# A two-layer hybrid backbone on one core: the order of its first loads, joined gate projections, and the list scheduler's price of a matmul

## The chip, the cores and the metric

One core of a Trainium2 chip runs the whole program in one launch. The metric is the device time of a run in microseconds; the median of several runs counts. Engines are named as in the profile: PE (TensorE, matmuls), PEld (its weight loads), DVE (VectorE), ACT (ScalarE), POOL (GpSimd) and SP (SyncE, which issues all DMAs here).

## What is computed

A stream of 256 latent tokens with a prefix of 256 context tokens passes two layers of width 1024. Cut to what matters here:

```
mod = silu(c) @ w_mod + b_mod                 # shift, scale, gate; context has its own
h   = rms(x) * (1 + scale) + shift            # 512 tokens
xa, ga, q, k, v, gb, qd, kvd, kr, gc, gm = split(h @ w_in)
ya = gated linear recurrence of xa            # both directions
yb = chunked retention of q, k, v             # both directions, 4 heads
yc = latent attention from qd, kvd, kr        # 8 heads
z  = sum over branches of sigmoid(gm_i) * ((y_i * silu(g_i)) @ w_down_i)
x  = x + gate * (z @ w_out)                   # the last layer: latent tokens only
```

## The kernel before

**Arithmetic.** Each operand of a large matmul is split into two fp32r parts, a rounded one and a remainder: `split` (lines 506 to 508) writes the rounded part on ACT and the remainder on DVE. `mm3` (520) then issues three matmuls for each product: high by high, high by low, low by high. Weights come as tiles of 128 x 1024 through `load_raw` and `load` (527 to 537): a DMA into a `raw` tile (5 slots), then the split into `whi` and `wlo` (5 slots each). The normalized activations live in `hh` and `hl`, each 128 x 8 x 512 (channel block, token).

**The order of the work.** The program is not emitted as it is written. `Recorder` (151) records every operation of all five engines with its dependencies and the price that `_cost` (412) gives it; `schedule` (224) then plays a list scheduler over these prices: on each engine the first ready operation in program order whose tiles have slots starts, and the order so found is emitted by line 368, which is why every row of the profile has that line. Tiles of a pool (`t2`, 21 slots of 128 x 1024; `sm`, 6 of 128 x 512; `mm`, the 8 PSUM banks) may be taken out of turn only if `RESERVE` slots stay free and the tile is at most `WINDOW` ahead (lines 39 and 40, test at 282 to 284). SP is one queue in the order of the list.

**The start** (lines 1167 to 1194). `mod_pe` (586) computes one of four blocks of the modulation: four DMAs of 512 KB into `raw` tiles, eight matmuls with a stationary operand of 32 columns, a copy out of the bank on ACT, four small matmuls with `sel`, and the DVE steps of `put_columns`. `load_x` brings 128 tokens, and `norm_begin` (652) squares, sums and scales them. `norm_channels` (678) transposes one block of channels of all tokens, applies scale and shift and splits the result into `hh` and `hl`. `kv_project` (753) multiplies two channel blocks by their latent weights of 320 columns into four banks. The program order is: block 0 of the modulation, four token loads, block 1, then for each of four pairs of channel blocks the normalization, the projection, and the modulation two blocks ahead.

**Projections for latent tokens only.** `proj` (689) computes 128 channels for all 512 tokens, or, with `lat`, for the 256 latent tokens: 24 matmuls of 256 columns. In layer 1 `silu_gate` (697; kinds gc, ga, gb, 8 each) and `ret_head` (1080; q, 2 for each of 4 heads) call it so. The readers take the result out of the bank: tanh on ACT and a product on DVE in `silu_gate`, the rope products on DVE in `ret_head`. `merge_rows` (996) keeps two `sm` tiles of gates while it runs 48 matmuls.

Of the kernel before, what the change touches and what calls it, by code (L numbers as in the profile page):

```python
# [36 lines left out]
LATENCY = (650.0, 300.0, 200.0)  # L37
SWITCH = 600
WINDOW = {"t2": 12, "sm": 24, "st": 24, "mm": 32}
RESERVE = {"t2": 3, "sm": 1, "st": 4, "mm": 1}  # L40
NRAW = 5
NHI = 5
# [108 lines left out]
class Recorder:  # L151
# [72 lines left out]
    def schedule(self):  # L224
# [34 lines left out]
        while left:  # L259
            progressed = True  # L260
            while progressed:
                progressed = False
                for e in engines:
                    if busy[e] > t:
                        continue
                    w = wait[e]
                    while w and w[0][0] <= t:
                        _, pr, k, op = heapq.heappop(w)
                        heapq.heappush(avail[e], (pr, k, op))
                    a = avail[e]  # L270
                    hold = []
                    pick = None
                    while a:
                        item = heapq.heappop(a)
                        op = item[2]
                        ok = True
                        need = {}
                        for b in op.allocs:
                            if b.live:
                                continue  # L280
                            need[b.tag] = need.get(b.tag, 0) + 1
                            spare = RESERVE.get(b.tag, 0) if b.seq > nxt[b.tag] + need[b.tag] - 1 else 0
                            if free[b.tag] < need[b.tag] + spare or b.seq > nxt[b.tag] + WINDOW.get(b.tag, 0):
                                ok = False
                        if ok and pick is not None:
                            if not switch(op):
                                hold.append((pick.prio, id(pick), pick))
                                pick = op
                                break
                            ok = False  # L290
                        elif ok:
                            pick = op
                            if not switch(op):
                                break
                            limit = op.prio + SWITCH
                            continue
                        hold.append(item)
                        if pick is not None and item[0] > limit:
                            break
                    for item in hold:  # L300
                        heapq.heappush(a, item)
                    if pick is None:
                        continue
                    op = pick
                    for b in op.allocs:
                        if not b.live:
                            b.live = True
                            free[b.tag] -= 1
                            q = self.tags[b.tag]["queue"]
                            while nxt[b.tag] < len(q) and q[nxt[b.tag]].live:  # L310
                                nxt[b.tag] += 1
                    cost = op.cost
                    if switch(op):
                        cost += 1283.0
                        table[0] = op.table
                    op.start = t
                    busy[e] = t + cost
                    op.end = t + cost + op.lag
                    order.append(op)
                    left -= 1  # L320
                    evn += 1
                    heapq.heappush(events, (busy[e], evn, None))
                    evn += 1
                    heapq.heappush(events, (op.end, evn, op))
                    for s in op.succs:
                        if s.engine == e and e != "SP":
                            s.ready = max(s.ready, busy[e] + SELF[e])
                        else:
                            s.ready = max(s.ready, op.end + _latency(e, s.engine))
                        s.npred -= 1  # L330
                        if s.npred == 0:
                            heapq.heappush(wait[s.engine], (s.ready, s.prio, id(s), s))
                            evn += 1
                            heapq.heappush(events, (s.ready, evn, None))
                    progressed = True
            if not left:
                break
            if not events:
                self.stuck(nxt, free, wait, avail)
            t2, _, op = heapq.heappop(events)  # L340
            t = max(t, t2)
            batch = [op]
            while events and events[0][0] <= t:
                batch.append(heapq.heappop(events)[2])
            for op in batch:
                if op is not None:
                    for b in op.bufs:
                        b.users -= 1
                        if b.users == 0:
                            free[b.tag] += 1  # L350
# [61 lines left out]
def _cost(engine, method, args, kwargs):  # L412
    out = args[0]
    n = _size(out) if isinstance(out, View) else 0
    if engine == "PE":
        if method == "transpose":
            return 107.0, 0.0
        passes = 1 if args[1].buf.dtype == F32R else 4
        return max(passes * n / 2.4, 27.0 if passes == 1 else 211.0) + 2.7, 0.0
    if engine == "SP":  # L420
        size = 4 * int(np.prod(args[1].shape))
        return size / 370.0 + 30.0, 2000.0
    psum = any(isinstance(x, View) and x.buf.psum for x in args[1:])
    if engine == "ACT":
        ptr = sum(isinstance(kwargs.get(k), View) for k in ("scale", "bias"))
# [22 lines left out]
def tile_hybrid(ctx, tc, ins, out):  # L448
# [8 lines left out]
        return p  # L457

    const = pool("const", 1)
    pool("hp", 1, ["hh", "hl"])  # L460
    pool("raw", NRAW)
    pool("whi", NHI)
    pool("wlo", NLO)
# [12 lines left out]
    def big(dt=F32R):  # L476
        return rec.tile("t2", [128, 1024], dt)
# [52 lines left out]
        return raw[:, 0:n]  # L530

    def load(src, n=1024):
        raw = load_raw(src, n)
        hi = rec.tile("whi", [128, 1024], F32R)[:, 0:n]
        lo = rec.tile("wlo", [128, 1024], F32R)[:, 0:n]
        split(hi, lo, raw)
        return hi, lo
# [45 lines left out]
        ng = col(l, "ng", s.start, 2).unsqueeze(2).to_broadcast([128, 2, 2])  # L583
        V.scalar_tensor_tensor(gt[:, s, :], src[:, 2:4, :], 1.0, ng, op0=ALU.add, op1=ALU.mult)

    def mod_pe(l, c, gt, sh):
        ps = bank()
        for kp in range(4):
            raw = load_raw(ins["wmod"][l, 4 * c + kp])
            for kk in range(2):  # L590
                k = 2 * kp + kk
                q = 32 * (k % 4)
                T.matmul(ps[q:q + 32, :], cz[:, k, :], raw[:, kk * 512:(kk + 1) * 512], start=k < 4, stop=k >= 4)
# [90 lines left out]
        V.tensor_scalar(hf[:, 256:512], pt[:, 256:512], gt[:, kt, 0:1], sh[:, kt, 0:1], op0=ALU.mult, op1=ALU.add)  # L684
        split(hh[:, kt, :], hl[:, kt, :], hf)

    hcur = [None, None]

    def proj(ps, l, kind, j, lat):
        hh, hl = hcur  # L690
        hi, lo = unit(l, kind, j)
        c = slice(256, 512) if lat else slice(0, 512)
        ps = ps[:, 0:256] if lat else ps
        mm3(ps, [(hi[:, k * 128:(k + 1) * 128], lo[:, k * 128:(k + 1) * 128], hh[:, k, c], hl[:, k, c]) for k in range(8)])
        return ps

    def silu_gate(l, kind, j):
        ps = proj(bank(), l, kind, j, l == 1)
# [34 lines left out]
    class Latents:  # L733
# [3 lines left out]
            self.q0 = 0 if l == 0 else 256  # L737
            self.kv_banks, self.q_banks = {}, {}

        def project(self, src, n, banks, tts, kps):  # L740
            hh, hl = hcur
            for kp in kps:
                hi, lo = load(ins[src][self.l, kp], 2 * n)
                for tt in tts:
                    if tt not in banks:
                        banks[tt] = bank()
# [3 lines left out]
                        w = slice(kk * n, (kk + 1) * n)  # L750
                        mm3(banks[tt][:, 0:n], [(hh[:, k, s], hl[:, k, s], hi[:, w], lo[:, w])], start=k == 0, stop=k == 7)

        def kv_project(self, kps):
            self.project("wkv", 320, self.kv_banks, range(NTT), kps)

        def q_project(self, kps):
            self.project("wqd", 384, self.q_banks, self.qtt, kps)
# [237 lines left out]

    def merge_rows(l, br, zr, first, last):
        names = {0: ("gmc", "dc"), 1: ("gma", "da"), 2: ("gmb", "db")}[br]
        hh, hl = hcur
        ys = ys_out[br]
        for c in range(2):  # L1000
            cs_ = slice(c * 512, (c + 1) * 512)
# [57 lines left out]
        return dt  # L1059

    def ret_pair(l, p):
        hh, hl = hcur
        banks = [bank() for _ in range(NTT)]
        for kp in range(4):
            hi, lo = unit(l, "v", 4 * p + kp)
# [100 lines left out]

    xt = []
    mods = {}
    hh = rec.tile("hh", [128, 8, 512], F32R)
    hl = rec.tile("hl", [128, 8, 512], F32R)  # L1170
    hcur[0], hcur[1] = hh, hl

    def new_mod():
        return rec.tile("gt", [128, 8, 2], F32), rec.tile("sh", [128, 8, 2], F32)
# [1 line left out]
    gt, sh = new_mod()  # L1176
    xn = {}

    def load_x(tt):
        x = big(F32)  # L1180
        S.dma_start(x, ins["xin"][tt])
        xn[tt] = norm_begin(x)

    lat = Latents(0, None)
    mod_pe(0, 0, gt, sh)
    for tt in range(NTT):
        load_x(tt)
    mod_pe(0, 1, gt, sh)
    for c in range(4):
        for kt in (2 * c, 2 * c + 1):  # L1190
            norm_channels(xn, kt, gt, sh, hh, hl)
        lat.kv_project((c,))
        if c < 2:
            mod_pe(0, c + 2, gt, sh)
    lat.tabs = rope_tables(0)
    sp = cload("sp", [128, DEPTH, 24])
    rrope = cload("rrope", [128, 2, 256])
# [41 lines left out]
    for l in range(DEPTH):  # L1239
# [43 lines left out]
        if l == 0:  # L1283
            for tt in tts:
                x = big(F32)
                S.dma_start(x, ins["xin"][tt])
                xt.append(x)
            hh = rec.tile("hh", [128, 8, 512], F32R)
            hl = rec.tile("hl", [128, 8, 512], F32R)

        def residual(half, tt, ps):
            hs = slice(half * 512, (half + 1) * 512)
# [25 lines left out]
                for half in range(2):  # L1318
                    norm_half(xn, tt, half, gt, sh, hh, hl)
        if l == 0:  # L1320
            hcur[0], hcur[1] = hh, hl
            lat = Latents(1, rope_tables(1))
            lat.kv_project(range(4))

# [113 lines left out]
```

## Time and profile before

| | |
|---|---|
| runs | 1401.82, 1403.86, 1404.72 us; median 1403.86 |
| profiled execution | 1403.3 us; its span 1401.4 us |
| PE busy | 1381.6 us (99%) |
| DVE busy | 1018.2 us (73%) |
| ACT busy | 792.1 us (57%) |
| mean DMA rate over the span | 121 GB/s |

The span runs from the first to the last instruction. Matmuls are pipelined: the duration of one contains the wait for the one ahead, so the distance between starts, not the duration, is what one costs in a row.

### The profile page before, as it was taken

The numbers are of one execution on the slowest core, as the hardware profiler recorded it, in microseconds if no ns is written. First come the engines' busy times: TensorE is split into PE (matmuls) and PEld (weight loads), VectorE is DVE, ScalarE is ACT, GpSimd is POOL, SyncE is SP. The second block draws the span as 40 slices with busy tenths as digits, with TensorE's granted clock in tenths as the row PEclk, the third lists the DMA queues.
The fourth block names the chain that finished last, engine by engine and source line by source line (L and its number), as shares of the span: only waits on it lengthen the run. The fifth ranks groups of instructions, "written<-read, shape, count | busy, mean of one in ns | idle before, by whom it ended". The sixth has DMA issues, their size and how long they took to land.

```text
span 1401.4 us, 19672 instructions
## 1 busy us (share of the span) xinstructions
PE 1381.6 (99%) x7182; PEld 1178.8 (84%) x7182; DVE 1018.2 (73%) x2035; ACT 792.1 (57%) x1565; POOL 83.6 (6%) x109
## 2 busy tenths in 40 slices
PE   6999999999999999999999999999999999999998
PEld 4888888888888888888888888999888888889887
DVE  3589887667668655574785765899777888878654
ACT  3585664676668323153433225877586877954442
POOL 0131110000000000010000001322000000000000
PEclk9999999999999999999999999999999999999999
DMA  8512212333333433413344452332343444556562
GB/s 313 189 48 78 68 46 68 98 89 99 91 114 120 150 87 104 134 60 105 108 140 151 124 185 72 116 99 91 99 123 118 154 130 139 162 176 203 145 185 76
DMA packets 51071, 170.17 MB, mean 121 GB/s; under 512 B 6048, under 2 KB 7840, under 8 KB 50976
## 3 DMA queue, kind: packets, MB, share of 16 engines
q1 hardware_dynamic: 50976, 168.93, 38.9%
q8 instruction: 56, 0.92, 0.3%
q14 instruction: 39, 0.32, 0.1%
HBM read 167.86 MB, written 1.05 MB: 121 GB/s over the span
## 4 chain that ended last, share of the span: by engine, by line
PE 93%; DVE 3%; DMA 2%; ACT 1%; issue 0%; SPq 0%; POOL 0%; ACTq 0%; POOLq 0%
PE mm L368 93%; DVE sm L368 1%; DVE t L368 1%; DVE wlo L368 1%; DMA raw<-in_wkv_dram 1%; ACT t L368 1%; DMA t<-in_xin_dram 1%; DMA raw<-in_wmod_dram 0%; DVE st L368 0%; DMA raw<-in_wqd_dram 0%; ACT whi L368 0%; SPq L368 0%; ACT sm L368 0%; POOL st L368 0%; ACT hh L368 0%
## 5 line engine op out<-in xcount | busy, mean ns | idle before, releaser
L368 ACT CAST whi<-raw 128x1024 fp32r<-128x1024 f32 (+4 forms) x280 | 275.6, 995 | 347.0 <-PE mm L368 294.8
L368 DVE TENSOR_TENSOR wlo<-raw,whi 128x1024 fp32r<-128x1024 f32 (+4 forms) x280 | 318.6, 1143 | 148.7 <-ACT whi L368 146.6
L368 PE MATMUL mm<-hh,whi 128*128 128x512 f32 (+1 forms) x960 | 349.7, 364 | 0.0
L368 PE MATMUL mm<-hh,wlo 128*128 128x512 f32 (+1 forms) x960 | 348.5, 363 | 0.0
L368 PE MATMUL mm<-hl,whi 128*128 128x512 f32 (+1 forms) x960 | 348.1, 363 | 0.0
L368 PE MATMUL mm<-whi,t 128*128 128x512 f32 (+1 forms) x656 | 208.3, 383 | 0.4 <-DVE t L368 0.4
L368 PEld LDWEIGHTS mm<-hl,whi 128*128 128x128 f32 x960 | 181.2, 189 | 26.7
L368 PEld LDWEIGHTS mm<-hh,wlo 128*128 128x128 f32 x960 | 181.2, 189 | 26.6
L368 PEld LDWEIGHTS mm<-hh,whi 128*128 128x128 f32 x960 | 181.2, 189 | 26.4
L368 PE MATMUL mm<-t,whi 128*128 128x512 f32 x512 | 160.1, 390 | 0.1
L368 POOL TENSOR_TENSOR st<-st,nhalf 128x2 f32<-128x2 f32 (+2 forms) x102 | 82.7, 817 | 1230.0 <-DVE st L368 1211.6
L368 PE MATMUL mm<-t,t 128*128 128x256 f32 (+1 forms) x912 | 153.8, 310 | 0.5 <-ACT t L368 0.5
L368 PEld LDWEIGHTS mm<-t,t 128*128 128x128 f32 x912 | 129.4, 190 | 11.7 <-DVE t L368 1.2
L368 PEld LDWEIGHTS mm<-whi,t 128*128 128x128 f32 x656 | 121.8, 188 | 18.8 <-DVE t L368 0.6
L368 PE MATMUL mm<-wlo,t 128*128 128x512 f32 (+1 forms) x328 | 125.6, 383 | 0.0
L368 PE MATMUL mm<-whi,hh 128*128 128x512 f32 (+2 forms) x336 | 123.8, 369 | 0.1
L368 PE MATMUL mm<-wlo,hh 128*128 128x512 f32 (+2 forms) x336 | 123.4, 368 | 0.0
L368 PE MATMUL mm<-whi,hl 128*128 128x512 f32 (+2 forms) x336 | 123.1, 369 | 0.2 <-DVE hl L368 0.2
L368 PEld LDWEIGHTS mm<-t,whi 128*128 128x128 f32 x512 | 95.8, 188 | 20.9 <-ACT t L368 0.8
L368 ACT ACTIVATE sm<-mm 128x128 f32<-128x128 f32 (+4 forms) x266 | 93.1, 366 | 21.3 <-PE mm L368 18.2
L368 ACT CAST t<-sm 128x256 fp32r<-128x256 f32 (+1 forms) x128 | 60.3, 487 | 71.2 <-DVE sm L368 67.7
L368 PE MATMUL mm<-t,wlo 128*128 128x512 f32 x256 | 99.6, 389 | 0.0
(108 smaller groups left out, 1738.4 us busy)
## 6 DMA issues: line engine op xcount, KB each, us to landing
raw<-in_wu_dram SPq DMA_DIRECT2D x224, 512.0 KB, 3.6
raw<-in_wmod_dram SPq DMA_DIRECT2D x48, 512.0 KB, 4.2
t<-in_xin_dram SPq DMA_DIRECT2D x8, 512.0 KB, 7.4
raw<-in_wup_dram SPq DMA_DIRECT2D x8, 512.0 KB, 4.0
raw<-in_wlru_dram SPq DMA_DIRECT2D x16, 256.0 KB, 3.2
raw<-in_wqd_dram SPq DMA_DIRECT2D x8, 384.0 KB, 3.3
raw<-in_wup_dram SPq DMA_DIRECT2D x8, 384.0 KB, 3.4
raw<-in_wkv_dram SPq DMA_DIRECT2D x8, 320.0 KB, 5.4
```

Of the source, the lines that this page charges most:

```text
L368: getattr(eng[op.engine], op.method)(*[r(x) for x in op.args], **{k: r(v) for k, v in op.kwargs.items()})
```

## The change

Four parts. (1) At the start the four token loads come first; then for each block its four modulation loads, now into slots of `t2`, and its latent weights, and then the block's work: modulation, two channel blocks, projection. (2) A projection with `lat` uses one tile `hx` that holds `hh` and `hl` side by side: the high weights meet both halves in one matmul of 2 x 256 columns, the low weights meet `hh` in one of 256, and the two halves of the bank are added by a copy on ACT and an addition on DVE into an `sm` tile. (3) `_cost` prices a one-pass matmul at columns / 2.4 + 13.3 ns with a floor of 108, counts a stationary operand of up to 32 columns as one pass, and a DMA byte at 1/400 ns. (4) Banks before number 24 are taken out of turn only if four stay free.

```diff
+FIRST = {"mm": 4}
-spare = RESERVE.get(b.tag, 0) if b.seq > nxt[b.tag] + need[b.tag] - 1 else 0
+spare = (FIRST if b.tag == "mm" and b.seq < 24 else RESERVE).get(b.tag, 0) if b.seq > nxt[b.tag] + need[b.tag] - 1 else 0
...
-        passes = 1 if args[1].buf.dtype == F32R else 4
-        return max(passes * n / 2.4, 27.0 if passes == 1 else 211.0) + 2.7, 0.0
+        passes = 1 if args[1].buf.dtype == F32R or _size(args[1]) <= 32 else 4
+        return max(passes * (n / 2.4 + 13.3), 108.0 if passes == 1 else 211.0), 0.0
     if engine == "SP":
         size = 4 * int(np.prod(args[1].shape))
-        return size / 370.0 + 30.0, 2000.0
+        return size / 400.0 + 30.0, 2000.0
...
-    pool("hp", 1, ["hh", "hl"])
+    pool("hp", 1, ["hx"])
...
-        c = slice(256, 512) if lat else slice(0, 512)
-        ps = ps[:, 0:256] if lat else ps
-        mm3(ps, [(hi[:, k * 128:(k + 1) * 128], lo[:, k * 128:(k + 1) * 128], hh[:, k, c], hl[:, k, c]) for k in range(8)])
-        return ps
+        if not lat:
+            mm3(ps, [(hi[:, k * 128:(k + 1) * 128], lo[:, k * 128:(k + 1) * 128], hh[:, k, :], hl[:, k, :]) for k in range(8)])
+            return ps
+        both = ps.rearrange("p (s t) -> p s t", s=2)
+        for k in range(8):
+            w = slice(k * 128, (k + 1) * 128)
+            if k > 0:
+                T.matmul(ps[:, 0:256], lo[:, w], hh[:, k, 256:512], start=False, stop=False)
+            T.matmul(both, hi[:, w], hx[:, :, k, 256:512], start=k == 0, stop=k == 7)
+            if k == 0:
+                T.matmul(ps[:, 0:256], lo[:, w], hh[:, k, 256:512], start=False, stop=False)
+        s = small()[:, 0:256]
+        A.copy(s, ps[:, 256:512])
+        V.tensor_tensor(s, ps[:, 0:256], s, op=ALU.add)
+        return s
...
-            raw = load_raw(ins["wmod"][l, 4 * c + kp])
+            raw = wm[c][kp]
...
-    mod_pe(0, 0, gt, sh)
     for tt in range(NTT):
-        load_x(tt)
-    mod_pe(0, 1, gt, sh)
+        xs.append(big(F32))
+        S.dma_start(xs[tt], ins["xin"][tt])
+    wm = {}
     for c in range(4):
+        wm[c] = [big(F32) for _ in range(4)]
+        for kp in range(4):
+            S.dma_start(wm[c][kp], ins["wmod"][0, 4 * c + kp])
+        wkv = load_raw(ins["wkv"][0, c], 640)
+        if c == 0:
+            for tt in range(NTT):
+                xn[tt] = norm_begin(xs[tt])
+        mod_pe(0, c, wm, gt, sh)
         for kt in (2 * c, 2 * c + 1):
             norm_channels(xn, kt, gt, sh, hh, hl)
-        lat.kv_project((c,))
-        if c < 2:
-            mod_pe(0, c + 2, gt, sh)
+        lat.kv_project((c,), {c: wkv})
```

`project` takes the weights loaded ahead through `split_raw`, the second half of `load`.

## Rows read from the trace of the kernel before

**Rows 1.** The page, part 4: the chain that ended last, by engine.

```profile
PE 93%; DVE 3%; DMA 2%; ACT 1%; issue 0%; SPq 0%; POOL 0%; ACTq 0%; POOLq 0%
```

**Rows 2.** Busy time by stretch: stretch, length, engines (instructions), PE clock, DMA share, GB/s.

```profile
0.00:48.30 48.30, 34.26 (x194) 21.59 (x194) 19.67 (x55) 20.03 (x35) 3.16 (x11) 0.93 0.87 316
...
90.00:131.00 41.00, 40.12 (x227) 33.49 (x225) 39.69 (x128) 25.91 (x94) 8.87 (x9) 1.00 0.28 79
131.00:1396.00 1265.00, 1264.73 (x6509) 1083.98 (x6510) 929.10 (x1760) 714.45 (x1321) 59.87 (x74) 1.00 0.38 117
```

**Rows 3.** Groups of PE by form, 0 to 48.3 us: count, busy us, mean ns.

```profile
L368 PE MATMUL mm<-raw,cz 128*32 128x512 f32 x64 | 13.3, 729 | 7.8 <-DMA raw<-in_wmod_dram 6.2 <-ACT hh L368 1.6
L368 PE MATMUL mm<-whi,hh 128*128 128x320 f32 x24 | 7.8, 325 | 0.1
...
L368 PE MATMUL mm<-ident,t 128*128 128x128 f32 x26 | 5.2, 360 | 4.3 <-DVE st L368 3.0 <-ACT sm L368 1.3
L368 PE MATMUL mm<-sel,sm 128*128 128x2 f32 x32 | 4.8, 270 | 1.2 <-ACT sm L368 1.2
```

**Rows 4.** Timeline of the opening: start us, duration us, instruction, count, idle before.

```profile
23.02 1.14 ACT L368 CAST hh<-sm 128x512 fp32r<-128x512 f32 x2 [0.91 <-DVE sm L368]
...
32.96 0.58 ACT L368 COPY sm<-mm 128x512 f32<-128x512 f32 x1 [2.86 <-PE mm L368]
...
34.57 0.95 PE L368 MATMUL mm<-sel,sm 128*128 128x2 f32 x8
...
36.02 0.54 DVE L368 TENSOR_SCALAR sm<-mm,gt,sh 128x256 f32<-128x256 f32 x1
36.04 0.31 PE L368 MATMUL mm<-whi,hh 128*128 128x320 f32 x1
...
37.07 0.31 PE L368 MATMUL mm<-wlo,hh 128*128 128x320 f32 x1
...
37.45 1.92 PE L368 MATMUL mm<-raw,cz 128*32 128x512 f32 x16
```

**Rows 5.** Timeline, weight loads that waited for the first modulation tiles.

```profile
7.34 0.19 PEld L368 LDWEIGHTS mm<-raw,cz 128*32 128x32 f32 x4 [0.97 <-DMA raw<-in_wmod_dram]
...
9.89 0.18 PEld L368 LDWEIGHTS mm<-raw,cz 128*32 128x32 f32 x4 [1.08 <-DMA raw<-in_wmod_dram]
```

**Rows 6.** Busy time by stretch of 5 us; the last two numbers are DMA share and GB/s.

```profile
10.00:15.00 5.00, 2.02 (x12) 1.11 (x10) 1.33 (x4) 3.72 (x7) 1.11 (x2) 0.84 1.03 417
15.00:20.00 5.00, 5.00 (x26) 3.80 (x27) 2.34 (x8) 2.16 (x6) 1.10 (x2) 0.50 1.02 403
20.00:25.00 5.00, 3.37 (x24) 1.47 (x18) 3.03 (x5) 2.35 (x4) 0.00 (x0) 0.97 0.69 240
...
40.00:45.00 5.00, 2.85 (x15) 2.09 (x16) 3.64 (x6) 4.07 (x8) 0.00 (x0) 1.00 1.00 349
```

**Rows 7.** Timeline of the SP queue: start us, us, DMA issues and their count.

```profile
20.57 1.75 SPq L368 DMA_DIRECT2D raw<-in_wmod_dram  x4
...
33.47 5.41 SPq L368 DMA_DIRECT2D raw<-in_wkv_dram  x2
```

**Rows 8.** Timeline of PE: matmuls of 512 columns (310 us), of 256 (1044 us).

```profile
309.71 0.39 PE L368 MATMUL mm<-hh,whi 128*128 128x512 f32 x1
...
311.52 0.39 PE L368 MATMUL mm<-hh,wlo 128*128 128x512 f32 x1
...
1044.01 0.28 PE L368 MATMUL mm<-hl,whi 128*128 128x256 f32 x1
...
1050.97 0.28 PE L368 MATMUL mm<-hh,wlo 128*128 128x256 f32 x1
```

**Rows 9.** Groups by form, whole span: 256-column reads of a bank, ACT and DVE.

```profile
L368 ACT ACTIVATE sm<-mm 128x256 f32<-128x256 f32 x32 | 12.4, 388 | 3.2 <-PE mm L368 3.1
...
L368 DVE TENSOR_TENSOR t<-mm,t 128x256 fp32r<-128x256 f32 x56 | 23.2, 417 | 1.8 <-ACT t L368 1.5
```

**Rows 10.** Busy time by stretch, in the attention of layer 1.

```profile
940.00:960.00 20.00, 20.00 (x129) 18.23 (x128) 19.39 (x54) 14.96 (x55) 3.54 (x4) 1.00 0.43 133
```

More of the change, by code (lines that the diff above doesn't have):

```diff
@@ L532, in load, with split_raw @@
     def load(src, n=1024):
-        raw = load_raw(src, n)
+        return split_raw(load_raw(src, n), n)
+    def split_raw(raw, n):
         hi = rec.tile("whi", [128, 1024], F32R)[:, 0:n]
@@ L584, in put_columns, with mod_pe @@
         V.scalar_tensor_tensor(gt[:, s, :], src[:, 2:4, :], 1.0, ng, op0=ALU.add, op1=ALU.mult)
-    def mod_pe(l, c, gt, sh):
+    def mod_pe(l, c, wm, gt, sh):
         ps = bank()
         for kp in range(4):
-            raw = load_raw(ins["wmod"][l, 4 * c + kp])
+            raw = wm[c][kp]
             for kk in range(2):
@@ L685, in norm_channels @@
         split(hh[:, kt, :], hl[:, kt, :], hf)
-    hcur = [None, None]
+    hcur = [None, None, None]
     def proj(ps, l, kind, j, lat):
-        hh, hl = hcur
+        hh, hl, hx = hcur
         hi, lo = unit(l, kind, j)
-        c = slice(256, 512) if lat else slice(0, 512)
-        ps = ps[:, 0:256] if lat else ps
-        mm3(ps, [(hi[:, k * 128:(k + 1) * 128], lo[:, k * 128:(k + 1) * 128], hh[:, k, c], hl[:, k, c]) for k in range(8)])
-        return ps
+        if not lat:
[13 more added lines that the diff above has]
+        return s
     def silu_gate(l, kind, j):
@@ L738, in __init__, with project @@
             self.kv_banks, self.q_banks = {}, {}
-        def project(self, src, n, banks, tts, kps):
-            hh, hl = hcur
+        def project(self, src, n, banks, tts, kps, raws=None):
+            hh, hl, hx = hcur
             for kp in kps:
-                hi, lo = load(ins[src][self.l, kp], 2 * n)
+                hi, lo = split_raw(raws[kp], 2 * n) if raws else load(ins[src][self.l, kp], 2 * n)
                 for tt in tts:
@@ L751, in project, with kv_project @@
                         mm3(banks[tt][:, 0:n], [(hh[:, k, s], hl[:, k, s], hi[:, w], lo[:, w])], start=k == 0, stop=k == 7)
-        def kv_project(self, kps):
-            self.project("wkv", 320, self.kv_banks, range(NTT), kps)
+        def kv_project(self, kps, raws=None):
+            self.project("wkv", 320, self.kv_banks, range(NTT), kps, raws)
         def q_project(self, kps):
@@ L997, in merge_rows @@
         names = {0: ("gmc", "dc"), 1: ("gma", "da"), 2: ("gmb", "db")}[br]
-        hh, hl = hcur
+        hh, hl, hx = hcur
         ys = ys_out[br]
@@ L1061, in ret_pair @@
     def ret_pair(l, p):
-        hh, hl = hcur
+        hh, hl, hx = hcur
         banks = [bank() for _ in range(NTT)]
@@ L1168, in tile_hybrid @@
     mods = {}
-    hh = rec.tile("hh", [128, 8, 512], F32R)
-    hl = rec.tile("hl", [128, 8, 512], F32R)
-    hcur[0], hcur[1] = hh, hl
+    hx = rec.tile("hx", [128, 2, 8, 512], F32R)
+    hh, hl = hx[:, 0], hx[:, 1]
+    hcur[0], hcur[1], hcur[2] = hh, hl, hx
     def new_mod():
@@ L1177, in tile_hybrid @@
     xn = {}
[L1179 to L1182, printed above, removed]
     lat = Latents(0, None)
-    mod_pe(0, 0, gt, sh)
+    xs = []
     for tt in range(NTT):
-        load_x(tt)
-    mod_pe(0, 1, gt, sh)
+        xs.append(big(F32))
+        S.dma_start(xs[tt], ins["xin"][tt])
+    wm = {}
     for c in range(4):
+        wm[c] = [big(F32) for _ in range(4)]
[6 more added lines that the diff above has]
+        mod_pe(0, c, wm, gt, sh)
         for kt in (2 * c, 2 * c + 1):
             norm_channels(xn, kt, gt, sh, hh, hl)
-        lat.kv_project((c,))
-        if c < 2:
-            mod_pe(0, c + 2, gt, sh)
+        lat.kv_project((c,), {c: wkv})
     lat.tabs = rope_tables(0)
@@ L1287, in tile_hybrid @@
                 xt.append(x)
-            hh = rec.tile("hh", [128, 8, 512], F32R)
-            hl = rec.tile("hl", [128, 8, 512], F32R)
+            hx = rec.tile("hx", [128, 2, 8, 512], F32R)
+            hh, hl = hx[:, 0], hx[:, 1]
         def residual(half, tt, ps):
@@ L1320, in tile_hybrid @@
         if l == 0:
-            hcur[0], hcur[1] = hh, hl
+            hcur[0], hcur[1], hcur[2] = hh, hl, hx
             lat = Latents(1, rope_tables(1))
```

## The prediction

> **What bounds the kernel now.** I read the chain of waits first, by engine [rows 1]: matmuls are 93% of it, so only what shortens TensorE's work or its gaps counts. Then a table of stretches [rows 2]. From 131 to 1396 us TensorE is busy 1264.73 of 1265 us: no order of the list can win anything there, only lose. The first 48.3 us are different: 34.26 us busy, at a granted clock of 0.93, which is 2.4 GHz but for some 6.8 us at 1.2 GHz. From 90 to 131 us VectorE is busy 39.69 of 41 us, and the chain runs over it.
>
> "Busy" overstates TensorE in the opening, as matmuls overlap, so I count work instead. By 48.33 us it has done 64 records of the modulation matmuls, 24 x 3 = 72 of the latent projection (the row shown is one of three alike), 32 of the selector and 26 of the 32 transposes [rows 3]. Undisturbed steps, from starts in rows 4: 16 modulation records take 1.92 us, 0.12 each; seven steps of 320 columns take 37.07 - 36.04 = 1.03, 0.147 each; 8 selector records take 0.95, 0.12 each; a transpose stands at 0.107 in the price function, and I take that. Sum: 64 x 0.12 + 72 x 0.147 + 32 x 0.12 + 26 x 0.107 = 7.7 + 10.6 + 3.8 + 2.8 = 24.9 us. TensorE is 48.3 - 24.9 = **23.4 us behind** what it could have done, and from there on it hardly stops.
>
> Why: modulation tiles come at 1.25 to 1.3 us (the weight loads at 7.34 and 9.89 us that waited for them are two tiles apart [rows 5]). The DMA engines are full until 20 us at 403 to 417 GB/s, then fall to 240 [rows 6]. The SP queue shows it: the third four modulation loads start only at 20.57 us, the last latent weights between 33.47 and 38.9 [rows 7]. All go through the five raw slots.
>
> **The opening, changed.** No load is added. The four token loads go ahead of the first modulation loads, each block's four modulation loads and its latent weights follow, and the modulation tiles take slots of the 21-slot pool instead of the raw ones. The table loads (rope, decay) fall behind all blocks; their readers come after the blocks too. On SP nothing in the row needs a slot that is late: 4 token tiles, 4 normalized ones and 16 modulation tiles are 24 for 21 slots, so the last three loads wait for token tiles, which are free some 3 us after they land at about 10 (square, power, scaling; an estimate), when more than 13 us of transfers are still queued. Token loads 5 us earlier bring the squares (ACT), powers (POOL) and scalings (DVE) forward into idle time.
>
> Bytes: 20 x 0.524 + 4 x 0.328 = 11.8 MB. The fourth 0.524 MB load landed at 9.89 us; the other 9.7 MB at 0.524/1.275 = 0.411 MB per us take 23.6 us. Last modulation tile at 32.7, last latent weights at 33.5 us. Behind that tile come four records (0.5), the copy (0.58), the selectors (0.95), 0.50 until the affine step starts, the affine step (0.54), and one rounding (1.14/2 = 0.57) [rows 4]: 3.6 us, with handoffs and other work on these engines 4.8. So the last block's projection starts at 37.5 us, and the query weights, next in the queue, keep TensorE fed from there. Its work by then: 24.9 plus six transposes (0.6) = 25.5. It is 12.0 us behind instead of 23.4: **11.4 us less**. Bounds: with 18 of the first query matmuls of 384 columns, at the planner's own 173 ns, filling the wait, 14.5 less; with transfers at 349 GB/s, the rate at 40 to 45 us [rows 6], 27.8 instead of 23.6 us, 4.2 less gain; and if the lower clock level falls on two blocks' projections (48 x 0.147 = 7 us) with nothing to hide it, 7 us less. So 0 to 14.5.
>
> I keep 10 of the 11.4: the stretch of 90 to 131 us, where VectorE is full, should move forward as a whole, as VectorE has over half of the first 48.3 us free [rows 2], but the late blocks now press more work of ACT and VectorE into fewer microseconds.
>
> **Joined gates.** `proj` with lat serves 32 projections in layer 1 (gc, ga, gb, 8 each, and 8 for q). Each has 24 matmuls of 256 columns; 58 steps from 1044.01 to 1050.97 us are 0.120 us each. The joined form has 8 of 256 and 8 of 512 columns; eight steps from 309.71 to 311.52 are 0.226 each [rows 8]. Per pair of joined matmuls 2 x 0.120 - 0.226 = 0.014 us, x 256 = **3.5 us less** on the bounding engine. The moving operand now reads two runs, one in each half of `hx`, which no row shows: if that costs what separate matmuls cost, 0 is gained; nothing suggests more. I take 2.8, near the row's end.
>
> The Trainium skill (TensorE: Matmul & The Clock Gate, Back-to-back issue gap) puts the gap of isolated matmuls at columns / 2.4 plus about 2.5 ns: by that, joining saves only 2.5 ns each, an estimated 0.6 us in all. The trace differs: 0.120 and 0.226 us leave 13 ns fixed, and the measurement decides.
>
> Added: 32 copies out of a bank (0.388 us by the 32 reads alike) and 32 additions (0.417) [rows 9]: 12.4 us on ACT and 13.3 on VectorE. TensorE doesn't wait for these while banks are free; the bank is free after the addition, about as early as before, when tanh and the product read it. Cover: in 940 to 960 us VectorE is 19.39 of 20 us busy [rows 10]. Eight of the projections lie in that region, 8 x 0.42 = 3.3 us; without cover all of it would count. I take 0.5, since TensorE has other projections to run. Net of gates: 2.3 less.
>
> **Prices.** The planner took a 512-column matmul for 216 ns and now takes 226.6, a 256-column one for 109 and now 120: the rows' values. A modulation matmul falls from 856 to 227 (two records, 0.24). The floor of 108 touches no matmul here (the one-pass ones have 256 columns or more) and a transpose stays at 107. So the opening is no longer planned with 32 x 0.63 = 20 us of matmul time that isn't there, which lets the better loads take effect. Between 131 and 1396 us it can't gain; a worse order can lose. I take 0 and leave the loss to the range and the last rival. The bank reserve of 4 before number 24 keeps four banks for the latent sums: no instruction. `hx` for `hh` and `hl`: the same bytes, the same last readers: 0.
>
> **Sum.** The profiled execution took 1403.3 us (1401.4 of span, 1.9 around it). 1403.3 - 10 - 2.3 = 1391.0; the runs' median is 0.56 above the profiled time: **1391.5 us**. Its own range is 1386 to 1396.
>
> **Rivals.**
> *Slow stream or cold engine.* The opening's loads run at 349 GB/s, or half clock stretches the blocks: 4 to 6 us of the 10 are lost, 1396.5. For it: the later full stretch of the queue is at that rate; against: 10 us at 403 to 417. Chance 0.12. The Trainium skill (DMA: Bandwidth & Descriptors, Specifications) gives about 358 GB/s as HBM's share per core, an estimated 3.5 us more for the 9.7 MB; the trace, one core alone at 417, disagrees so far.
>
> *VectorE takes it back.* The opening ends 10 us earlier, but the stretch to 131 us is held by VectorE's 39.69 of 41 us and ends where it did, or two or three earlier. Then 1403.9 - 2.3 - 1.5 = 1400. Against: its work there depends on what TensorE delivers earlier. Chance 0.12.
>
> *Small tiles run out (slower).* The joined projection holds a small tile, the query pair of a retention head two, beside three of its rope step: five of six. In layer 1 the merge holds two through 48 matmuls, 48 x 0.226 = 10.8 us. If TensorE's projections then stand with no free bank at each of the four heads, up to 4 x 10.8 = 43 us are lost; it decides from 12.3/4 = 3.1 us per head. At 4 us per head: 1391.5 + 16 = 1407.5. Against: the list knows the tiles and can put other projections there. Chance 0.08.
>
> *The change misses its aim.* The list puts the new loads in a row, but order elsewhere gives up what the opening gains: 1401 to 1404. Chance 0.08.
>
> **Numbers.** The forecast has 0.6. The range 1384 to 1401 takes in the first two rivals and the bounds (14.5 + 3.5 less on one side). A measurement of this kernel can tell about 0.2%, 2.8 us, from no change: faster is below 1401.05, slower above 1406.7. Faster: 0.6 + 0.12 + two thirds of 0.12 = 0.80; slower 0.08; the rest, 0.12, within.
>
> **What would show it.** Right: tokens land by 10 us, the DMA stays near 410 GB/s to 32 us, the last modulation tile lands near 33 us and the last block's projection starts near 37; joined pairs step 0.226 + 0.120; stretches after 131 us keep TensorE at 100%; the layer-1 stretch is 2 to 3 us shorter. Wrong: SP standing on the 21-slot pool before 25 us; steps of 0.24 or more at joined matmuls; TensorE idle behind VectorE in 80 to 130 us; idle TensorE at the four retention heads of layer 1.

## The result: slower, and the profile after

The changed kernel takes 1413.13 us (median of 4 runs, 1412.91 to 1415.39), the kernel before 1403.54 beside it: a ratio of 1.0073, with a 95% interval of 1.0055 to 1.0090. The forecast was 1391.5, with a range of 1384 to 1401: wrong in sign. The profiled execution spans 1410.5 us, 9.1 more than before.

The page of the changed kernel, busy time by engine and, from its part 4, the chain by engine:

```profile
PE 1382.9 (98%) x6926; PEld 1161.2 (82%) x6926; DVE 1027.7 (73%) x2067; ACT 800.3 (57%) x1597; POOL 83.9 (6%) x109
...
PE 78%; DVE 9%; ACT 7%; DMA 3%; issue 1%; POOL 1%; SPq 0%; ACTq 0%; DVEq 0%; POOLq 0%
```

TensorE has 256 matmuls fewer (6926 for 7182), as the joined gates make it. But the chain, 93% matmuls before [rows 1], is 78% now: ACT and VectorE hold 16% of it. The stretches of the changed kernel show where:

```profile
0.00:48.30 48.30, 36.04 (x222) 24.05 (x223) 22.46 (x60) 22.38 (x38) 3.61 (x11) 1.00 0.90 338
...
90.00:131.00 41.00, 38.26 (x223) 32.44 (x222) 39.62 (x141) 24.69 (x89) 7.89 (x8) 1.00 0.22 66
...
200.00:600.00 400.00, 398.86 (x1832) 330.44 (x1831) 264.30 (x407) 213.41 (x297) 2.78 (x5) 1.00 0.34 104
...
850.00:1250.00 400.00, 396.96 (x2076) 338.67 (x2075) 331.42 (x680) 306.54 (x643) 32.77 (x38) 1.00 0.39 120
```

From 90 to 131 us TensorE has lost 1.9 us of busy time against [rows 2], and in the body, where nothing was idle before, it now is: 1.1 us of 400 and 3.0 of 400. It waits in many short gaps. What it waited for between 200 and 1390 us, first in the kernel before, then in the changed one (total us, times, longest):

```profile
PEld mm L368 <- ACT t L368: 0.8, 2, 0.4
PEld mm L368 <- DVE t L368: 0.5, 1, 0.5
PEld mm L368 <- DVE sm L368: 0.4, 2, 0.2
```

```profile
PEld mm L369 <- ACT t L369: 6.5, 12, 1.1
PEld mm L369 <- DVE t L369: 4.8, 12, 0.9
PEld mm L369 <- ACT sm L369: 3.3, 5, 1.8
```

One of these gaps in the changed kernel's timeline:

```profile
454.64 0.68 DVE L369 TENSOR_TENSOR sm<-sm,t 128x512 f32<-128x512 f32 x1
454.77 0.19 PEld L369 LDWEIGHTS mm<-hx,wlo 128*128 128x128 f32 x1
454.99 0.39 PE L369 MATMUL mm<-hx,wlo 128*128 128x512 f32 x1
...
455.36 0.62 ACT L369 CAST t<-sm 128x512 fp32r<-128x512 f32 x1 [2.29 <-DVE sm L369]
456.03 0.19 PEld L369 LDWEIGHTS mm<-t,whi 128*128 128x128 f32 x1 [1.07 <-ACT t L369]
456.03 0.50 PE L369 MATMUL mm<-t,whi 128*128 128x512 f32 x1 [0.65 <-ACT t L369]
```

A product leaves VectorE at 455.32, ACT rounds it until 455.98, and the matmul that the list has put next on TensorE starts at 456.03, 0.8 us late.

Busy time hides most of this, so the working below uses **lag**, the measure of the prediction's opening: the time t less the undisturbed steps of all matmuls begun before t. The steps are the medians between starts in a row in the traces: 0.227 us for 512 columns, 0.174 for 384, 0.147 for 320, 0.120 for 256, 0.109 for a transpose and 0.112 for a selector; for a modulation record it is a mean, 16 of them in 1.92 us, 0.120. They add up to 1366.2 us before and 1362.9 with joined gates. Each column is one profiled execution. Lag in us, for the main kernels of the next section ("changed, old matmul price" is f1_oldmm there, "fastest" h1_ahead):

| at us | before | changed | opening alone | joined alone | prices alone | changed, old matmul price | fastest |
|---|---|---|---|---|---|---|---|
| 50 | 23.6 | 19.4 | 24.6 | 24.5 | 22.6 | 19.4 | 15.8 |
| 80 | 23.9 | 19.5 | 25.8 | 25.3 | 24.8 | 19.6 | 15.9 |
| 200 | 27.8 | 28.0 | 30.9 | 29.3 | 33.0 | 23.7 | 20.0 |
| 600 | 28.5 | 31.0 | 30.8 | 29.9 | 36.5 | 23.8 | 20.0 |
| 850 | 28.8 | 31.1 | 31.1 | 30.2 | 36.8 | 23.9 | 20.2 |
| 1350 | 30.2 | 42.6 | 32.5 | 32.6 | 45.7 | 26.5 | 22.9 |

The changed kernel is 4.4 us ahead at 80 us, has given that back by 200, and loses 14.6 us from 200 to 1350 where the kernel before loses 2.4. With 3.3 us less work, 12.4 - 3.3 = 9.1 us: the difference of the spans. The joined gates alone stand 1.4 us worse than the kernel before at 80 us already, though they lie in layer 1: in that execution the granted clock was 0.91 over the first 60 us, in the kernel before 0.94.

### The profile page after: what moved, and what is told of

Its sections match the earlier page's. It is cut to its first block, busy times and chain, and to the rows that moved or that the text cites. A ratio compares the mean times of both kernels' runs of the same rounds, so it can differ in the third digit from the quotient of the medians.

```text
span 1410.5 us, 19235 instructions
## 1 busy us (share of the span) xinstructions
PE 1382.9 (98%) x6926; PEld 1161.2 (82%) x6926; DVE 1027.7 (73%) x2067; ACT 800.3 (57%) x1597; POOL 83.9 (6%) x109
## 3 DMA queue, kind: packets, MB, share of 16 engines
HBM read 167.86 MB, written 1.05 MB: 120 GB/s over the span
## 4 chain that ended last, share of the span: by engine, by line
PE 78%; DVE 9%; ACT 7%; DMA 3%; issue 1%; POOL 1%; SPq 0%; ACTq 0%; DVEq 0%; POOLq 0%
PE mm L369 78%; DVE t L369 4%; ACT t L369 3%; DVE sm L369 3%; DVE wlo L369 2%; ACT whi L369 2%; DMA t<-in_wmod_dram 1%; ACT sm L369 1%; DVE st L369 1%; POOL st L369 1%; DMA sm<-in_grope_dram 1%; DMA raw<-in_wu_dram 0%; ACT L369 0%; DMA t<-in_xin_dram 0%; DMA raw<-in_wmod_dram 0%
## 5 line engine op out<-in xcount | busy, mean ns | idle before, releaser
L369 PE MATMUL mm<-hx,whi 128*128 128x512 f32 x1664 | 534.3, 393 | 1.7 <-ACT sm L369 0.9
L369 PEld LDWEIGHTS mm<-hx,whi 128*128 128x128 f32 x1664 | 309.8, 188 | 62.8 <-DVE t L369 1.4
L369 PE MATMUL mm<-hx,wlo 128*128 128x512 f32 (+1 forms) x960 | 343.1, 363 | 0.0
L369 PEld LDWEIGHTS mm<-hx,wlo 128*128 128x128 f32 x960 | 180.4, 188 | 28.5
L369 PE MATMUL mm<-whi,hx 128*128 128x512 f32 (+2 forms) x672 | 197.0, 369 | 1.5 <-ACT hx L369 1.4
L369 PEld LDWEIGHTS mm<-whi,hx 128*128 128x128 f32 x672 | 122.8, 188 | 21.5 <-ACT hx L369 3.9
L369 PE MATMUL mm<-wlo,hx 128*128 128x512 f32 (+2 forms) x336 | 122.9, 368 | 0.1
L369 PEld LDWEIGHTS mm<-t,whi 128*128 128x128 f32 x512 | 95.2, 188 | 25.8 <-ACT t L369 5.2
L369 ACT ACTIVATE sm<-mm 128x128 f32<-128x128 f32 (+4 forms) x242 | 85.7, 375 | 16.7 <-PE mm L369 16.3
L369 ACT ACTIVATE sm<-mm,st 128x256 f32<-128x256 f32 (+2 forms) x86 | 49.8, 592 | 47.2 <-DVE st L369 38.7
L369 DVE SCALAR_TENSOR_TENSOR t<-raw,cf,t 128x512 f32<-128x512 f32 x98 | 69.6, 743 | 9.6 <-DMA raw<-in_wmod_dram 9.5
```

Source lines behind the costliest of these rows:

```text
L369: getattr(eng[op.engine], op.method)(*[r(x) for x in op.args], **{k: r(v) for k, v in op.kwargs.items()})
```

## The experiments

All times are medians in us; the ratio is to the kernel before in the same set of runs, with its 95% interval.

| run | time | ratio |
|---|---|---|
| opening alone (e1_open) | 1406.32 | 1.0019 (1.0009 to 1.0028) |
| joined gates alone (e2_join) | 1400.40 | 0.9980 (0.9970 to 0.9989) |
| prices and bank reserve alone (e3_price) | 1418.05 | 1.0098 (1.0083 to 1.0113) |
| all but the prices (e4_noprice) | 1404.18 | 1.0000 (0.9991 to 1.0010) |
| all, old matmul price (f1_oldmm) | 1396.77 | 0.9942 (0.9927 to 0.9957) |
| matmul and DMA price alone (f2_pm) | 1426.80 | 1.0154 (1.0138 to 1.0169) |
| all, handoff to TensorE doubled (f3_lat) | 1405.72 | 1.0016 (1.0006 to 1.0026) |
| all, half the fixed part (f4_half) | 1401.24 | 0.9981 (0.9971 to 0.9991) |
| all, matmul prices x 0.953 (g1_uniform) | 1399.69 | 0.9969 (0.9958 to 0.9980) |
| all, ACT and VectorE prices x 1.05 (g2_others) | 1399.33 | 0.9966 (0.9955 to 0.9978) |
| all, fixed part 13.0 (g4_jit) | 1413.21 | 1.0068 (1.0053 to 1.0083) |
| f1_oldmm, projection a block later (h1_ahead) | 1392.56 | 0.9922 (0.9907 to 0.9937) |
| all, only the modulation's price new (k1_pz) | 1396.18 | 0.9935 (0.9918 to 0.9951) |
| h1_ahead, matmul price 5% lower still (k2_low) | 1397.95 | 0.9952 (0.9937 to 0.9966) |

**Which part.** Each of the three parts alone on the kernel before, and the change without its prices.

Opening alone: the hunks of the start, `split_raw` and `FIRST`.

> The kernel before with the new opening (loads in a row, work by block, the bank reserve) alone; old prices, separate gate matmuls. Theory P (the new prices' order loses what the rest gains): the opening alone keeps its gain, about 4 us, so near 1399. Theory J (the joined gates lose it in layer 1): the same, 1399, as neither is in this kernel. Theory O (the opening's gain is taken back by VectorE before 200 us, as in the changed kernel): 1403, no change.

Joined gates alone: the hunk of `proj`, with `hx`.

> The kernel before with the joined gate projections alone. Theory J: slower by 5 to 8 us, 1409 to 1412, all of it behind 850 us. Theory P: faster by 1 to 3 us, 1401 to 1402, since TensorE's work is 3 us less. Theory O: the same as P.

Prices alone:

```diff
+FIRST = {"mm": 4}
...
-        passes = 1 if args[1].buf.dtype == F32R else 4
-        return max(passes * n / 2.4, 27.0 if passes == 1 else 211.0) + 2.7, 0.0
+        passes = 1 if args[1].buf.dtype == F32R or _size(args[1]) <= 32 else 4
+        return max(passes * (n / 2.4 + 13.3), 108.0 if passes == 1 else 211.0), 0.0
...
-        return size / 370.0 + 30.0, 2000.0
+        return size / 400.0 + 30.0, 2000.0
```

> The kernel before with the new prices and the bank reserve alone. Theory P: slower by 5 to 9 us, 1409 to 1412, TensorE losing it in small gaps over the span. Theory J and theory O: within 2 us of 1403.5.

The changed kernel with the three price lines put back:

> The changed kernel with the old prices. Theory P: most of the loss goes, 1395 to 1400, under the kernel before. Theory J: stays at 1410 to 1414. Theory O: 1404 to 1409.

The prices alone cost 14.6 us (1418.05 to 1403.45), theory P's side and more than it asked. The joined gates alone gain what they were to gain: theory J falls. The opening alone does not gain, it costs 2.9 us: no theory had that. Opening and gates together without the prices are even (1404.18); only theory O's range, 1404 to 1409, holds that, and O falls with the cost of the prices alone. P was right on the body (lag gained from 200 to 1350 us: 12.6 with the prices, 1.6 with the opening, 3.3 with the gates, 2.4 before), but the opening needs something of the prices too.

What the joined form costs: the added additions, then the added copies, in two fences for two views of the changed kernel (groups by form of VectorE, of ACT); then starts within one projection in the fastest kernel's timeline:

```profile
L369 DVE TENSOR_TENSOR sm<-mm,sm 128x256 f32<-128x256 f32 x32 | 13.2, 414 | 0.0
```

```profile
L369 ACT COPY sm<-mm 128x256 f32<-128x256 f32 x32 | 11.7, 369 | 0.1
```

```profile
1088.22 0.40 PE L369 MATMUL mm<-hx,whi 128*128 128x512 f32 x1
1088.45 0.28 PE L369 MATMUL mm<-hx,wlo 128*128 128x256 f32 x1
...
1089.96 0.39 PE L369 MATMUL mm<-hx,whi 128*128 128x512 f32 x1
```

Five pairs in 1.74 us are 0.348 each (the median over the run is 0.351), against 3 x 0.120 = 0.360: 9 to 12 ns less for each of 256 pairs, 2.3 to 3.1 us. The moving operand's two runs cost nothing to speak of.

**Why the exact price hurts.** The old price of a matmul lies 5% under the step at 512 columns (216 ns for 227) and 9% at 256 (109 for 120), the new one on it. Theory M: a price under the real one is slack. The list believes TensorE to be faster than it is, so it has the other engines deliver for a moment that TensorE reaches later; with the exact price their work is due just in time, and each deviation is a gap on the engine that bounds the kernel. Rivals: any other order moves the time at random (R), the modulation's price does it (Z), or the new ratio between short and long matmuls (S).

The changed kernel with the old matmul price:

```diff
-        return max(passes * (n / 2.4 + 13.3), 108.0 if passes == 1 else 211.0), 0.0
+        return max(passes * n / 2.4, 27.0 if passes == 1 else 211.0) + 2.7, 0.0
```

> The changed kernel, but a matmul priced as before (columns / 2.4 + 2.7 ns, about 5% too low); a modulation matmul stays at one pass, a DMA byte at 1/400. Theory M (a price below the real one lets the other engines deliver early, the exact price leaves no slack and the bounding engine then waits in many small gaps): the opening keeps its 4 us, the joined gates their 3, nothing is lost behind 200 us: 1395 to 1399. Theory R (any other order of the list moves the time by several us at random): anywhere from 1398 to 1415. Theory Z (the one-pass price of the modulation is what hurts): 1408 to 1413.

The kernel before with the matmul's and the DMA's new price, not the modulation's:

> The kernel before with the fixed part of the matmul's price and the DMA price only (modulation at four passes as before, old opening, separate gates, no bank reserve). Theory M: slower by 8 to 14 us, 1411 to 1418, in gaps between 200 and 600 and between 850 and 1250 us. Theory Z: 1402 to 1406. Theory R: no forecast, 1398 to 1418.

The changed kernel with more handoff time in the plan:

```diff
-LATENCY = (650.0, 300.0, 200.0)
+LATENCY = (1300.0, 300.0, 200.0)
```

> The changed kernel with the planner's handoff time to TensorE doubled from 650 to 1300 ns, the new prices kept. Theory M: slack put back by another way, so most of the loss behind 200 us goes: 1398 to 1405. Theory Z: 1410 to 1415, no help. Theory R: 1398 to 1415.

Half the fixed part:

```diff
-        return max(passes * (n / 2.4 + 13.3), 108.0 if passes == 1 else 211.0), 0.0
+        return max(passes * (n / 2.4 + 8.0), 108.0 if passes == 1 else 211.0), 0.0
```

> The changed kernel with a fixed part of 8.0 ns in place of 13.3, halfway to the old price. Theory M: between the two, 1400 to 1408, TensorE's loss between 200 and 1390 us about half of the changed kernel's. Theory Z: 1410 to 1415. Theory R: no order by dose, 1398 to 1415.

With the old matmul price alone put back the change is faster than the kernel before, 1396.77, and the waits between 200 and 1390 us are all but gone:

```profile
PEld mm L369 <- DVE sm L369: 0.5, 2, 0.3
PEld mm L369 <- ACT t L369: 0.3, 1, 0.3
```

The lag from 200 to 1350 us goes with the dose: 14.6 us at a fixed part of 13.3, 5.6 at 8.0, 2.8 at the old price. Doubled handoff time brings it to 9.0, and the time to 1405.72, just over M's range: slack of this other sort goes only part of the way. The matmul and DMA prices without the modulation's give 1426.80, worse than all three prices: Z falls, and f2_pm overshot M's 1418 too, since its opening also lost (lag 32.0 at 60 us; 23.5 before).

Three more for R and S. Matmul prices in the new ratios but 5% under the steps (the recorded expectation has transposes scaled too; they keep their 107 ns, as `_cost` returns that ahead of this line):

```diff
-        return max(passes * (n / 2.4 + 13.3), 108.0 if passes == 1 else 211.0), 0.0
+        return 0.953 * max(passes * (n / 2.4 + 13.3), 108.0 if passes == 1 else 211.0), 0.0
```

> The changed kernel with every matmul and transpose price (with its fixed part) times 0.953: the ratios between shapes are the new ones, all of them about 5% under the rows. Theory M (a price under the real one is slack): 1395 to 1400, no loss behind 200 us. Theory S (the ratio between 256 and 512 columns is what spoils the order, as the fixed part weighs more on short matmuls): 1409 to 1414.

Exact matmul prices, the two other engines 5% dearer:

```diff
             cost, lag = _cost(self.name, method, args, kwargs)
+            cost = cost * 1.05 if self.name in ("ACT", "DVE") else cost
```

> The changed kernel, matmul prices exact as changed, but every ACT and VectorE price 5% higher. Theory M: the slack comes back from the other side, 1396 to 1405. Theory S: 1409 to 1414.

And a fixed part of 13.0 for 13.3:

> The changed kernel with a fixed part of 13.0 ns in place of 13.3, so small that it adds no slack worth naming (0.1%), but every tie of the list can fall otherwise. Theory M: 1410 to 1415. Theory R (each new order of the list moves the time at random by several us): outside of that, 1397 to 1409 or over 1416.

S falls: with the new ratios between matmuls and prices 5% low the loss from 200 to 1350 us is 3.5 us. Slack from the other side does the same (4.0). And a change of price that adds no slack changes nothing: 1413.21 (13.6 us). Against R this last run says little alone, as its plan puts only 207 of 6878 TensorE operations at another place than the changed kernel's (2248 with the old price). What speaks against R is the whole set: the four kernels with the exact fixed part or 13.0 lose 12.6 to 14.6 us from 200 to 1350, doubled handoff 9.0, half the fixed part 5.6, and the others, all with a matmul price at least 5% low or the other engines' 5% high, 1.6 to 4.9. So it is the level of the bounding engine's price against the others'.

Were the others' prices low too, so that the exact price only broke a balance of equal errors? Hardly. The splits of the query weights in the changed kernel's timeline, three in a row and one alone:

```profile
39.88 2.30 ACT L369 CAST whi<-raw 128x768 fp32r<-128x768 f32 x3
...
40.74 2.69 DVE L369 TENSOR_TENSOR wlo<-raw,whi 128x768 fp32r<-128x768 f32 x3 [0.44 <-ACT whi L369]
...
42.85 0.83 ACT L369 CAST whi<-raw 128x768 fp32r<-128x768 f32 x1 [0.67 <-PE mm L369]
...
43.71 0.96 DVE L369 TENSOR_TENSOR wlo<-raw,whi 128x768 fp32r<-128x768 f32 x1 [0.28 <-ACT whi L369]
```

A step is (2.30 - 0.83) / 2 = 0.735 us on ACT, where `_cost` has 93 + 0.834 x 768 = 734 ns, and (2.69 - 0.96) / 2 = 0.865 on VectorE, where it has 869. Over all instructions of the changed kernel that follow one another without a pause, ACT's steps add up to 473.9 us for a price of 468.1, VectorE's to 720.0 for 700.6. So the other engines were priced 1 to 3% low; a small part of the loss may lie there.

**The opening.** In the changed kernel and in f1_oldmm the opening is 4 us ahead, not 11.4. The timeline of the changed kernel, TensorE, selectors and modulation of the third and fourth block and starts of projections:

```profile
35.18 0.95 PE L369 MATMUL mm<-sel,sm 128*128 128x2 f32 x8
...
36.55 1.92 PE L369 MATMUL mm<-t,cz 128*32 128x512 f32 x16
39.02 0.42 PE L369 MATMUL mm<-whi,hx 128*128 128x320 f32 x1 [0.55 <-ACT hx L369]
...
42.65 0.95 PE L369 MATMUL mm<-sel,sm 128*128 128x2 f32 x8
...
47.54 0.31 PE L369 MATMUL mm<-wlo,hx 128*128 128x320 f32 x1
```

In the view of all engines, ACT's copy of the fourth block's modulation:

```profile
39.40 0.58 ACT L369 COPY sm<-mm 128x512 f32<-128x512 f32 x1
```

The third block's projection starts at 39.02, the last one's at 47.3 (the row at 47.54 is its second kind of matmul). The fourth block's 16 modulation records are done by 38.5 and their copy by 40, but the selectors stand behind the whole projection of the third block, until 42.65; the affine steps and rounding follow. So a block takes some 8 us (selectors at 18.67, 27.84, 35.18, 42.65). To test it, the projection of a block was put behind the next block's chain, with the old matmul price:

```diff
+    wkv = {}
     for c in range(4):
...
-        wkv = load_raw(ins["wkv"][0, c], 640)
+        wkv[c] = load_raw(ins["wkv"][0, c], 640)
...
-        lat.kv_project((c,), {c: wkv})
+        if c > 0:
+            lat.kv_project((c - 1,), wkv)
+    lat.kv_project((3,), wkv)
```

> The changed kernel with the old matmul price (as the run that had it alone undone, 1396.8) and the latent projection of a block put behind the next block's modulation and normalization in program order. Theory C (the opening's blocks take 8 us each because each one's chain of copy, selector, affine step and rounding starts only when the projection of the block before is through): the last block's projection starts 3 to 6 us earlier than at 47 us and the time is 1391 to 1394. Theory L (the landing of the loads sets the blocks): 1396 to 1398, no change.

Theory C holds: the lag at 50 us falls from 19.4 to 15.8, the selectors start at 17.8, 23.3, 30.71 and 37.55, the last projection at 41.5 instead of 47.3. In the same view:

```profile
30.71 0.95 PE L369 MATMUL mm<-sel,sm 128*128 128x2 f32 x8
...
33.98 1.92 PE L369 MATMUL mm<-t,cz 128*32 128x512 f32 x16
...
37.55 0.95 PE L369 MATMUL mm<-sel,sm 128*128 128x2 f32 x8
```

At 1392.56 us it is the fastest kernel here, 11.2 us under the kernel before beside it and 20.6 under the changed one.

Two more runs. Of the prices only the modulation's (one pass up to 32 columns):

> The changed kernel with the old matmul price and the old DMA price (1/370); of the prices only the one-pass modulation matmul is left. Theory A (the new opening needs the modulation at its real price): within 1.5 us of 1396.8, the run that also has the new DMA price. Theory B (it needs the DMA price): back at 1402 to 1406, as with all old prices (1404.2).

And the fastest version with a matmul price lower still:

```diff
-        return max(passes * n / 2.4, 27.0 if passes == 1 else 211.0) + 2.7, 0.0
+        return max(0.95 * passes * n / 2.4, 27.0 if passes == 1 else 211.0) + 2.7, 0.0
```

> The fastest version so far (1392.6: old matmul price, projection behind the next block's modulation) with the matmul price lowered by another 5% (0.95 x columns / 2.4 + 2.7). Theory M with enough slack at the old price: 1391 to 1394, no change, as TensorE loses almost nothing behind 200 us any more. Rival: more slack also helps between 80 and 140 us, 1388 to 1390.5. Second rival: too low a price draws the other engines' work too far ahead and costs slots, 1395 to 1405.

The modulation's price is what the opening needs: 1396.18 with it, 1404.18 without, all else alike. The granted clock goes with it. The first 48.3 us without and with that price:

```profile
0.00:48.30 48.30, 33.09 (x175) 22.26 (x176) 19.73 (x52) 19.21 (x32) 3.17 (x11) 0.89 0.89 329
```

```profile
0.00:48.30 48.30, 37.23 (x224) 24.62 (x225) 22.65 (x60) 22.35 (x38) 3.16 (x11) 0.96 0.89 330
```

The clock is 0.89 without (also in the opening alone) and 0.96 with; which share of the 8 us comes by the lower clock was not separated. With the old price the list runs each block's modulation late; in the opening alone the last block's records start only here:

```profile
44.04 1.05 PE L369 MATMUL mm<-t,cz 128*32 128x512 f32 x4 [0.32 <-ACT sm L369]
48.77 1.91 PE L369 MATMUL mm<-t,cz 128*32 128x512 f32 x12
```

and its projection at 57.1. A further 5% off the matmul's price harms, by 5.4 us (4.7 when each is taken against the kernel before beside it), inside the range of the second rival on record: against h1_ahead 1.0 more lag by 80 us, 2.9 more between 100 and 140 and 2.1 between 1150 and 1250, where TensorE again waits, mostly for ACT and VectorE. So of the doses tried the old price is the best. Why too much slack brings the waits back, and whether it is the slots that the rival names, was not tried; that stays open.

## Why the prediction was wrong, step by step

**Prices: the step that failed.** "Between 131 and 1396 us it can't gain; a worse order can lose. I take 0 and leave the loss to the range and the last rival." The first half held, the 0 did not: the prices alone cost 14.6 us, and the fixed part is the cause. I compared the new prices with the rows, found them right, and took right for harmless. But the old price, 5 to 9% low, had been a margin on the engine that bounds the kernel, and the exact one took it away: 14.6 us of lag from 200 to 1350 us, 2.8 with the old price put back. The rival for it, "order elsewhere gives up what the opening gains", ended at 1404 with a chance of 0.08; it was the case, and reached 9 us further.

**The opening: mis-sized.** "So the last block's projection starts at 37.5 us": it started at 47.3. The stream was right to about 1 us: the last modulation tile landed at 33.9 us, forecast 32.7. The changed kernel's stretches, DMA share and GB/s last:

```profile
15.00:20.00 5.00, 4.29 (x28) 1.70 (x28) 1.03 (x3) 1.31 (x2) 0.00 (x0) 1.00 1.03 412
...
25.00:30.00 5.00, 4.31 (x29) 2.44 (x32) 1.00 (x5) 1.33 (x3) 0.00 (x0) 1.00 1.03 407
...
35.00:40.00 5.00, 4.45 (x37) 2.78 (x36) 4.07 (x12) 3.10 (x7) 0.00 (x0) 1.00 1.03 386
```

From 10 to 40 us the rate is 383 to 417 GB/s. The Trainium skill (DMA: Bandwidth & Descriptors, Specifications) has about 358 GB/s as a core's share of HBM; one core alone stays over it for 30 us here, and the measurement decides. What I left out was the chain of the blocks before the last: I counted 4.8 us behind the last tile as if the last block waited for nothing else, and 13.4 passed. Of these, 2.7 went by before its modulation matmuls could start (36.55), behind the work of the blocks ahead, 0.9 before ACT's copy (39.40) and 2.7 before the selectors (42.65), behind the projection of the block ahead; from the selectors to the projection it took 4.6. 11.4 us less lag became 4.2 to 4.4. With the projection put behind, it is 7.8 to 8.0.

**Joined gates: right.** Forecast 2.3 net; measured 3.1 (1403.45 to 1400.40), pairs at 0.348 to 0.351 for 0.346, copies 0.369 for 0.388, additions 0.414 for 0.417. The Trainium skill (TensorE: Matmul & The Clock Gate, Back-to-back issue gap) would have had, by an estimate, 0.6 us from its 2.5 ns per matmul; the trace has 9 to 12 ns for each pair, and the measurement decides.

**The rivals.** Slow stream: no. A cold engine: no; the granted clock of the first 48.3 us is 1.00, where it was 0.93 [rows 2]. VectorE takes it back: the changed kernel does lose its lead between 80 and 200 us (lag up 8.5 us, before 3.9), but with the old matmul price it is up 4.1 only, so this too was the price. Small tiles: no; the gates alone lose 3.3 us of lag from 200 to 1350, before 2.4.

## What to carry to other kernels

A price in a planner is not only an estimate but a margin: in this kernel a price some per cent under the real one, on the engine that bounds it, went with other engines that deliver in time, and putting it right cost more than the whole rest of the change brought. When a price is corrected, put the slack back, on that engine or as dearer prices of the others, and measure the dose in both directions, here 13.3, 8 and 2.7 ns, and 5% less. And a pipeline of blocks is sized by the longest chain of one block, including what its short steps queue behind, not by the landing of its last load.

## What the hardware showed unexpectedly

A long row of loads is not issued in a row. The SP queue of the changed kernel, and what SP waited for in the first 30 us:

```profile
2.12 1.85 SPq L369 DMA_DIRECT2D t<-in_xin_dram  x4
4.01 1.99 SPq L369 DMA_DIRECT2D t<-in_wmod_dram  x4
...
7.32 4.58 SPq L369 DMA_DIRECT2D t<-in_wmod_dram  x4
```

```profile
SPq L369 <- DMA t<-in_wmod_dram: 12.0, 13, 0.9
SPq L369 <- DMA t<-in_xin_dram: 2.8, 3, 1.4
```

The first eight 512 KB loads take about 0.5 us each to issue; from 7.32 us on each waits for the landing of an earlier one, the first of them though their slots were never used before. The semaphores in the trace's records show who asks for it: the program. Its loads use eight landing semaphores in turn, and each load waits for the one eight places ahead of it: that at 7.32 us for the second token load, landed at 7.31, that at 9.03 for the third, landed at 9.01. It cost nothing here, as the DMA engines stayed full.

The granted clock stayed at its upper level, 2.4 GHz, through the first 48.3 us of the changed kernel, although TensorE's busy time there is only 36.04 us, near the 34.26 of the kernel before, whose clock fell to 1.2 GHz for some 6.8 us. The sum over the stretch hides what came before the fall, at 13.4 us: from 10 to 14 us TensorE was busy 1.02 us in the kernel before and 3.51 in the changed one. The times of one kernel go with the clock too: of the 18 executions of the kernel before beside f1_oldmm, the three with a mean granted clock of 1.000 took 1400.96 to 1401.62 us, the eight with 0.995 or 0.996 took 1403.86 to 1405.82.
